# Shortening a decoder's opening from six to four plain tiles, and exchanging two of seven half products in every FFN

## The chip, the cores and the metric

The kernel runs on one core of one Trainium2 chip. The metric is the device time of one execution in microseconds (us), as a median of several runs. A core has five engines that run side by side, each through its own queue in order: PE (TensorE, matmuls and their weight loads), DVE (VectorE), ACT (ScalarE), POOL (GpSimd) and SP (SyncE, which here only issues DMAs). They wait for each other by semaphores.

## What is computed

A decoder trunk of two layers over 512 tokens of width 1024. Each layer has a SwiGLU FFN, a mixer and a second FFN, all with a residual and an RMSNorm ahead of them. Only the FFNs matter here, four in all:

```python
def swiglu(h, w_in, w_out):
    gate, up = jnp.split(h @ w_in, 2, axis=-1)
    return (jax.nn.silu(gate) * up) @ w_out
...
    for l in range(DEPTH):
        x = x + 0.5 * swiglu(rms_norm(x, ffn1_norm[l]), ffn1_w_in[l], ffn1_w_out[l])
        h = rms_norm(x, mix_norm[l]) @ w_mix_in[l]
        ...
        x = x + y @ w_mix_out[l]
        x = x + 0.5 * swiglu(rms_norm(x, ffn2_norm[l]), ffn2_w_in[l], ffn2_w_out[l])
```

The inner width is 2816, that is 22 tiles of 128. Everything is float32. A product is made from three matmuls of rounded parts (high by high, high by low, low by high; mm3, lines 392, 398, 399), so each operand is first split: ACT casts the high part (L378 or L841 for weights, L774/L779 for the moving side), then DVE subtracts it from the source for the low part (L379, L843, L775/L779).

## The kernel before

**An FFN has two stretches.** The first inner tiles are computed plainly while the norm is still being made: the *covered* tiles. Two tiles go together (four PSUM banks: gate and up of each), in four granules of 24 matmuls of 512 columns. Their results stay in the banks until DVE multiplies them by the inverse norm (clear, L643 and L644), ACT takes the silu and DVE the products (values). The opening FFN of layer 0 has six covered tiles, the three others four.

All further tiles go through `halved` (L781), a scheme of seven half products, P1 to P7, in place of eight. A unit is two inner tiles. Each product has 24 matmuls of 256 columns, and the products of a unit share three banks by their letter (L909 to L915):

```python
            new = ("P1", "P2", "P5")
            k = {"P2": "c", "P5": "b", "P3": "b"}.get(p, "a")
            if p in new:
                work[u, k] = bank(kind)
```

So P1, P6, P7 and P4 add into one bank, a; P5 and P3 into b; P2 has c. Between two products of one bank, ACT copies what stands there so far: after P1 (L933), after P6 (g2, L940), after P5 (L943). A product that adds to the bank has to wait for that copy, since it would change what is being read.

**What sets the order.** `plan` (L80) lists all products of an FFN in one order: the seven of each unit in ORDER_IN, and, from the second chunk of units on, products of the output weights (ORDER_OUT) between them by a written pattern. It also gives every DMA and every sum a step. `halved` runs through that list. For each product it emits, in this order: the matmuls; `prepare` of the product three places later (LEAD = 3), whose ACT cast comes first; the copy of the bank; the DVE subtraction of the prepared product; then what the plan and ENTRY have for this step. `follow` pins that order on each engine. The split weights of `prepare` lie in three buffers (tag hl, L839), so the cast for product n + 3 writes to the buffer that product n reads.

ENTRY (L45) is the table of what is emitted at which step around the change from covered tiles to half products: the norm, the normalised input (x), its sums (+), the operands P1 to P7, clears, silus and values. Steps 4 to 7 are the second covered pair's granules, and with four covered tiles, steps 8 to 10 belong to the preparation of the first three products, and step 11 + n follows product n.

Banks come from eight: mm (3), po (1), sc (2), pt (2). Pairs of tiles and units take the sets (mm, mm, mm, po) and (sc, sc, pt, pt) by turns; the units of an FFN take four banks in turn from one set.

**The opening.** At the start PE multiplies zeros (`idle`, L1743) while x and the first weights are on their way: two before x is transposed, one after. Each takes a new tile of the single po bank. The zeros come from a DVE memset (L215), the third of the DVE queue.

Of the kernel before, what the change touches and what calls it, by code (L numbers as in the profile page):

```python
# [8 lines left out]
F32 = mybir.dt.float32  # L9
F32R = mybir.dt.float32r  # L10
# [15 lines left out]
P = 128  # L26
T = 512
D = 1024
# [5 lines left out]
CHUNKS = ((0, 8), (8, 8), (16, 6))  # L34


ORDER_IN = ("P1", "P2", "P6", "P5", "P7", "P3", "P4")
ORDER_OUT = ("P2", "P1", "P5", "P6", "P7", "P3", "P4")
LEAD = 3

# [10 lines left out]
    },  # L51
# [5 lines left out]
    },  # L57
}

# [124 lines left out]
class Trunk:  # L184
# [8 lines left out]
    def __init__(self, ctx, tc):  # L193
        self.tc = tc
        self.nc = tc.nc
        nc = self.nc
        self.const = ctx.enter_context(tc.tile_pool(name="const", bufs=1))
        self.res = ctx.enter_context(tc.tile_pool(name="res", bufs=1))
        self.wp = ctx.enter_context(tc.tile_pool(name="wp", bufs=1))
        self.ps = ctx.enter_context(  # L200
            tc.tile_pool(name="ps", bufs=1, space=bass.MemoryType.PSUM)
        )
        self.dram = ctx.enter_context(
            tc.tile_pool(name="dram", bufs=1, space=bass.MemoryType.DRAM)
        )
        self.ident = self.const.tile([P, P], F32, tag="ident", name="ident")
        make_identity(nc, self.ident)
        self.ones_mean = self.const.tile([P, P], F32, tag="ones_mean", name="ones_mean")
        nc.vector.memset(self.ones_mean, 1.0 / D)
        self.epsc = self.const.tile([P, 1], F32, tag="epsc", name="epsc")  # L210
        nc.vector.memset(self.epsc, EPS)
        self.xT = self.res.tile([P, KD, T], F32, tag="xT", name="xT")

        self.none = self.res.tile([P, T], F32R, tag="inv", name="none")
        nc.vector.memset(self.none.bitcast(F32), 0.0)  # L215

        self.xh, self.xl = [None] * KD, [None] * KD
        self.uid = 0
        self.ntog = 0
        self.tab, self.tab_users = None, []  # L220
        self.chain = {}

    def build_consts(self, scratch):

# [402 lines left out]
    def cover(self, fp, w_in, w_out, covered, mean, begin):  # L627

        nc = self.nc
        if begin is not None:
            x, gain = begin
        A, V = (lambda i, e=e: self.follow(e, i) for e in "av")
        norm, tiles, values = [], [], {}
        halved = self.halved(fp, w_in, w_out, covered, lambda n: deal(n))

        def clear(t):

            gi = fp.tile([P, T], F32, tag="g2", name=self.n("gi"), bufs=2)  # L640
            ui = fp.tile([P, T], F32, tag="u2", name=self.n("ui"), bufs=2)
            pg, pu = tiles[t]
            V(nc.vector.tensor_mul(gi, pg, self.inv))  # L643
            V(nc.vector.tensor_mul(ui, pu, self.inv))  # L644
            values[t] = gi, ui

        def value(t):
            a, k = divmod(t, 4)
            gi, ui = values.pop(t)
            for b in range(2):  # L650
                V(self.hidden(
                    self.quarter(fp, 0, a, b)[:, k, :],
                    *(v[:, 256 * b : 256 * b + 256] for v in (gi, ui)), a != b,
                ))

        def squares():

            norm.append(self.bank("pt" if self.ntog % 2 == 0 else "po"))
            i = self.sum_norm(norm[0])
            if begin is None:  # L660
                self.follow("p", i)

        def deal(n):
            if n == mean and begin is None:
                squares()
            for what in filter(None, ENTRY[covered].get(n, "").split(", ")):
                name, *at = what.split()
                at = [int(v) if v.isdigit() else v for v in at]
                if name == "norm":
                    for e, i in self.take_norm(norm[0], fp):  # L670
                        self.follow(e, i)
                    self.table(SILU)
                    self.signs()
                elif name == "x":
                    self.normalise(fp, *at)
                elif name == "+":
                    x, y = (self.xn[tuple(v)] for v in (at[:2], at[2:]))
                    V(nc.vector.tensor_add(x, x, y))
                elif name == "clear":
                    clear(*at)  # L680
                elif name == "silu":
                    gi = values[at[0]][0]
                    A(self.act(gi, gi, AF.Silu))
                elif name == "values":
                    value(*at)
                elif name == "load":
                    next(halved)
                elif name == "sum":
                    self.first_sum()
                else:  # L690
                    self.operand(fp, name)

        for f in range(0, covered, 2):
            banks = self.next4()

            def parts(k, kk, f=f):
                r = slice(k * P, (k + kk) * P)
                return [w_in[r, f * P : (f + 2) * P], w_in[r, FF + f * P : FF + (f + 2) * P]]

            opening = f == 0 and begin is not None  # L700

            self.stream(
                [(bk, slice(c, c + P), None) for bk, c in zip(banks, (0, 256, 128, 384))],
                parts, self.xact, KD, None,
                (lambda *a: self.open_x(x, gain, fp, *a)) if opening else None,
                None if opening else (lambda k, f=f: deal(2 * f + k // 2)), begin is None or f > 2,

                lead=f == 2 and begin is not None,
            )
            tiles += [banks[:2], banks[2:]]  # L710
            if opening:
                nt = iter(["xh4", "xl4", "xh5", "xl5", "xh6", "xl6", "r2", "r3", "r4", "r5"])
                self.build_consts(lambda dt: fp.tile([P, T], dt, tag=next(nt), name=self.n("c")))

                squares()
        for _ in halved:
            pass
# [997 lines left out]
    def open_x(self, x, gain, fp, k, loaded=False):  # L1715

        if loaded is None:
            if k == 0:
                self.xb[1] = self.turn(self.xb[1], 1)
            self.norm_part(k + 1, fp, self.xb[k + 1], 0)  # L1720
            return
        if not loaded:
            if k == 0:
                self.idle(2)
                self.begin_norm(gain, fp)
                self.table(LNEXP)
                self.follow("a", self.tab_ins)
                self.xb = {0: self.load_x(x, 0, fp)}
                self.load_open(0)
                self.idle(1)  # L1730
                self.xb[1] = self.load_x(x, 1, fp, True)
                self.load_open(1)
            self.norm_part(k, fp, self.xb[k], 0)

            self.between = lambda *a: self.open_x(x, gain, fp, k, None)
            return
        for j in (k + 2, k + 3):
            if j < KD:
                self.xb[j] = self.load_x(x, j, fp)
        for j in (k, k + 1):  # L1740
            self.open_rest(j, fp)

    def idle(self, n):  # L1743

        for _ in range(n):
            b = self.bank("po")
            self.follow("p", self.nc.tensor.matmul(b, self.none[:, :P], self.none, start=True, stop=True))

    def open_rest(self, j, fp):
# [25 lines left out]
def trunk_kernel(  # L1775
# [4 lines left out]
    k = Trunk(ctx, tc)  # L1780
    for l in range(DEPTH):
        k.ffn(
            ffn1_w_in[l], ffn1_w_out[l], mix_norm[l], 4 if l else 6, 2,
            begin=(x, ffn1_norm[0]) if l == 0 else None,
        )
        k.mix(
            l, w_mix_in[l], w_mix_out[l], conv_w[l], hgrn_out_gain[l], fox_q_gain[l],
            fox_k_gain[l], fox_f_bias[l], ffn2_norm[l], hgrn_lb_logits,
        )
        k.ffn(  # L1790
            ffn2_w_in[l], ffn2_w_out[l], ffn1_norm[l + 1] if l + 1 < DEPTH else None, 4, 3,
            out=out if l + 1 == DEPTH else None,
        )
# [29 lines left out]
```

## Time and profile before

| | us |
|---|---|
| median of 3 runs | 1830.18 (1828.83 to 1830.91) |
| the profiled execution | 1832.37 |
| its span, first to last instruction | 1830.6 |
| PE busy | 1821.0 |
| DVE busy | 1445.3 |
| ACT busy | 1001.7 |
| POOL busy | 185.1 |

All times in the profile are of the one profiled execution, counted from the start of its span. A row of a timeline has the start, the time taken (from the first row's start to the last row's end where rows are merged), the engine, the line of the kernel, what is written and read, and in brackets the idle time before it with what ended it. Matmuls overlap: their starts, not their times taken, tell the pace. A row of the waits has who waited for whom, the total, how often, and the longest. In the rows of chains and waits, a name such as "ACT g L940" is the engine, the tile written and the line.

### The profile page before, as it was taken

The numbers are of one execution on the slowest core, as the hardware profiler recorded it, in microseconds if no ns is written. First come the engines' busy times: TensorE is split into PE (matmuls) and PEld (weight loads), VectorE is DVE, ScalarE is ACT, GpSimd is POOL, SyncE is SP. The second block draws the span as 40 slices with busy tenths as digits, with TensorE's granted clock in tenths as the row PEclk, the third lists the DMA queues.
The fourth block names the chain that finished last, engine by engine and source line by source line (L and its number), as shares of the span: only waits on it lengthen the run. The fifth ranks groups of instructions, "written<-read, shape, count | busy, mean of one in ns | idle before, by whom it ended". The sixth has DMA issues, their size and how long they took to land.

```text
span 1830.6 us, 31999 instructions
## 1 busy us (share of the span) xinstructions
PE 1821.0 (99%) x12934; PEld 1674.7 (91%) x12934; DVE 1445.3 (79%) x1965; ACT 1001.7 (55%) x1414; POOL 185.1 (10%) x190
## 2 busy tenths in 40 slices
PE   9999999999999999999999999999999999999999
PEld 7899999888888899999889999998888888999997
DVE  8889786679677888879678887976777778888883
ACT  5455554465666465555445555555656655555552
POOL 0011120100000101112001111201000001020210
PEclk9999999999999999999999999999999999999999
DMA  7668783242543767868276787823425438677762
GB/s 214 177 134 189 177 180 94 68 124 68 127 110 96 216 136 168 193 165 174 81 202 140 174 183 190 163 69 84 114 74 127 119 98 217 161 152 196 154 135 92
DMA packets 249908, 262.38 MB, mean 143 GB/s; under 512 B 19816, under 2 KB 228464, under 8 KB 249760
## 3 DMA queue, kind: packets, MB, share of 16 engines
q1 hardware_dynamic: 193904, 192.15, 35.7%
q0 software_dynamic: 55840, 68.19, 23.4%
q8 instruction: 101, 1.65, 0.4%
q14 instruction: 47, 0.39, 0.1%
q10 hardware_dynamic: 16, 0.00, 0.0%
HBM read 226.15 MB, written 2.17 MB: 125 GB/s over the span
## 4 chain that ended last, share of the span: by engine, by line
PE 96%; ACT 1%; DVE 1%; DMA 1%; issue 0%; SPq 0%; DVEq 0%; ACTq 0%
PE mm L392 14%; PE mm L399 14%; PE mm L398 14%; PE sc L392 6%; PE sc L399 6%; PE sc L398 6%; PE pt L392 6%; PE pt L399 6%; PE pt L398 6%; PE po L392 4%; PE po L399 4%; PE po L398 4%; PE sc L1600 1%; PE po L1655 1%; PE sc L1414 1%; PE pt L1637 1%
## 5 line engine op out<-in xcount | busy, mean ns | idle before, releaser
L841 ACT CAST hl<-w 128x1024 fp32r<-128x1024 f32 x322 | 337.7, 1050 | 347.6 <-PE mm L399 81.9
L843 DVE TENSOR_TENSOR hl<-w,hl 128x1024 fp32r<-128x1024 f32 x322 | 392.5, 1220 | 87.2 <-ACT hl L841 87.0
L379 DVE TENSOR_TENSOR hl<-st,hl 128x1024 fp32r<-128x1024 f32 (+3 forms) x152 | 160.0, 1053 | 120.4 <-ACT hl L378 119.7
L378 ACT CAST hl<-st 128x1024 fp32r<-128x1024 f32 (+3 forms) x152 | 138.6, 912 | 176.3 <-PE po L399 81.5
L392 PE MATMUL mm<-xc,hl 128*128 128x256 f32 (+1 forms) x730 | 201.4, 276 | 0.3 <-ACT g L940 0.3
L399 PE MATMUL mm<-xc,hl 128*128 128x256 f32 x728 | 201.4, 277 | 0.0
L398 PE MATMUL mm<-xc,hl 128*128 128x256 f32 x728 | 201.2, 276 | 0.0
L392 PE MATMUL sc<-xc,hl 128*128 128x256 f32 (+1 forms) x530 | 146.4, 277 | 0.6 <-ACT g L940 0.6
L399 PE MATMUL sc<-xc,hl 128*128 128x256 f32 x528 | 146.1, 277 | 0.0
L398 PE MATMUL sc<-xc,hl 128*128 128x256 f32 x528 | 146.0, 277 | 0.0
L392 PEld LDWEIGHTS mm<-xc,hl 128*128 128x128 f32 x730 | 137.0, 188 | 0.8 <-ACT g L940 0.5
L398 PEld LDWEIGHTS mm<-xc,hl 128*128 128x128 f32 x728 | 136.8, 188 | 0.0
L399 PEld LDWEIGHTS mm<-xc,hl 128*128 128x128 f32 x728 | 136.6, 188 | 0.1
L392 PE MATMUL pt<-xc,hl 128*128 128x256 f32 (+1 forms) x482 | 132.7, 276 | 0.0
L398 PE MATMUL pt<-xc,hl 128*128 128x256 f32 x480 | 132.7, 276 | 0.0
L399 PE MATMUL pt<-xc,hl 128*128 128x256 f32 x480 | 132.6, 276 | 0.0
L392 PE MATMUL mm<-x,hl 128*128 128x512 f32 x272 | 108.8, 400 | 0.0
L399 PE MATMUL mm<-x,hl 128*128 128x512 f32 x272 | 106.1, 390 | 0.0
L398 PE MATMUL mm<-x,hl 128*128 128x512 f32 x272 | 105.9, 389 | 0.0
L392 PEld LDWEIGHTS sc<-xc,hl 128*128 128x128 f32 x530 | 99.5, 188 | 1.5 <-ACT g L940 1.0
L399 PEld LDWEIGHTS sc<-xc,hl 128*128 128x128 f32 x528 | 99.2, 188 | 0.1
L398 PEld LDWEIGHTS sc<-xc,hl 128*128 128x128 f32 x528 | 99.1, 188 | 0.0
(487 smaller groups left out, 5470.6 us busy)
## 6 DMA issues: line engine op xcount, KB each, us to landing
w<-in_ffn_w_in_dram SPq DMA_DIRECT2D x140, 512.0 KB
w<-in_ffn_w_out_dram SPq DMA_DIRECT2D x64, 512.0 KB
w<-in_ffn_w_out_dram POOLq DMA_DIRECT2D x56, 512.0 KB, 9.0
st<-in_w_mix_in_dram SPq DMA_DIRECT2D x80, 256.0 KB
w<-in_ffn_w_in_dram POOLq DMA_DIRECT2D x39, 512.0 KB, 8.1
st<-in_ffn_w_in_dram SPq DMA_DIRECT2D x70, 256.0 KB
w<-S POOLq DMA_DIRECT2D x35, 512.0 KB, 4.7
st<-in_ffn_w_out_dram SPq DMA_DIRECT2D x24, 512.0 KB
```

The source lines that it names most:

```text
L378: a = nc.scalar.copy(hi, src[:, c : c + w])
L379: b = nc.vector.tensor_sub(lo, src[:, c : c + w], hi)
L392: i = nc.tensor.matmul(acc[:, c], ah, bh[:, c], start=first and c.start == 0, stop=False, skip_group_check=True,)
L398: nc.tensor.matmul(acc, ah, bl, start=False, stop=False, skip_group_check=True)
L399: i = nc.tensor.matmul(acc, al, bh, start=False, stop=last, skip_group_check=True)
L841: A(nc.scalar.copy(hi, src))
L843: return lambda: V(nc.vector.tensor_sub(lo, src, hi))
L1414: nc.tensor.matmul(s2[:, :, t], e[:, i * P : (i + 1) * P], e2[:, :, t], start=True, stop=True)
L1600: mm = lambda *a, **k: E(nc.tensor.matmul(*a, skip_group_check=True, **k))
L1637: E(nc.tensor.transpose(tb[:, k * P : (k + 1) * P], to[u][:, j * P : (j + 1) * P], self.ident))
L1655: E(nc.tensor.matmul(self.ob[:, o], half[2][:, j, h].rearrange("p a d -> p (a d)"), part[:, at[0] : at[-1] + 1, :].rearrange("p b t -> p ( ...
```

## The change

It has three parts.

1. *Opening:* layer 0's first FFN has four covered tiles, as the others have; two more tiles go through the half products. It gets a table of its own, "opening", later in its steps than that of the other FFNs: the norm at step 6 (in place of 5), P5's operand at 10, P6's at 11 with the sum that it is made of, P7's at 12, clear 0 at 9 and clear 1 at 11.
2. *Zeros:* four before x is transposed and three after, all of a call into one po bank, and the memset of the zeros comes first on DVE.
3. *Order:* ORDER_IN has P5 ahead of P6, in all four FFNs. ORDER_OUT stays.

```diff
-ORDER_IN = ("P1", "P2", "P6", "P5", "P7", "P3", "P4")
+ORDER_IN = ("P1", "P2", "P5", "P6", "P7", "P3", "P4")
...
-    6: {
-        7: "norm, x 0 0", 8: "x 1 0, clear 0, clear 1", 9: "silu 0, silu 1, x 0 1, P1, + 0 0 0 1",
-        10: "load, P2, values 0, values 1, x 1 1", 11: "P5, clear 2, + 0 0 1 1",
-        12: "silu 2, P6, clear 3, sum", 13: "values 2, silu 3, + 0 1 1 1, P3", 14: "P7, values 3, + 0 0 1 0",
-        15: "P4", 16: "clear 4", 17: "silu 4", 18: "values 4, clear 5", 19: "silu 5", 20: "values 5",
+    "opening": {
+        6: "norm", 7: "load, x 0 0, x 1 0, P1", 8: "x 0 1, + 0 0 0 1, P2", 9: "clear 0, sum",
+        10: "P5, x 1 1", 11: "+ 0 0 1 1, P6, clear 1", 12: "silu 0, + 0 1 1 1, P7", 13: "values 0, P3",
+        14: "silu 1, + 0 0 1 0, P4", 15: "values 1", 17: "clear 2", 18: "silu 2",
+        19: "values 2", 20: "clear 3", 21: "silu 3", 22: "values 3",
     },
...
+        self.none = self.res.tile([P, T], F32R, tag="inv", name="none")
+        self.follow("v", nc.vector.memset(self.none.bitcast(F32), 0.0))
...
-                self.idle(2)
+                self.idle(4)
...
-                self.idle(1)
+                self.idle(3)
...
     def idle(self, n):
 
+        b = self.bank("po")
         for _ in range(n):
-            b = self.bank("po")
             self.follow("p", self.nc.tensor.matmul(b, self.none[:, :P], self.none, start=True, stop=True))
...
-            ffn1_w_in[l], ffn1_w_out[l], mix_norm[l], 4 if l else 6, 2,
+            ffn1_w_in[l], ffn1_w_out[l], mix_norm[l], 4, 2,
```

The change also has `deal` read the new table where the FFN is the opening one.

More of the change, by code (lines that the diff above doesn't have):

```diff
@@ L196, in __init__ @@
         nc = self.nc
+        self.uid = 0
+        self.ntog = 0
+        self.tab, self.tab_users = None, []
+        self.chain = {}
         self.const = ctx.enter_context(tc.tile_pool(name="const", bufs=1))
@@ L208, in __init__ @@
         self.ones_mean = self.const.tile([P, P], F32, tag="ones_mean", name="ones_mean")
-        nc.vector.memset(self.ones_mean, 1.0 / D)
+        self.follow("v", nc.vector.memset(self.ones_mean, 1.0 / D))
         self.epsc = self.const.tile([P, 1], F32, tag="epsc", name="epsc")
@@ L212, in __init__ @@
         self.xT = self.res.tile([P, KD, T], F32, tag="xT", name="xT")
-        self.none = self.res.tile([P, T], F32R, tag="inv", name="none")
-        nc.vector.memset(self.none.bitcast(F32), 0.0)
         self.xh, self.xl = [None] * KD, [None] * KD
[L218 to L221, printed above, removed]
     def build_consts(self, scratch):
@@ L665, in deal @@
                 squares()
-            for what in filter(None, ENTRY[covered].get(n, "").split(", ")):
+            for what in filter(None, ENTRY[covered if begin is None else "opening"].get(n, "").split(", ")):
                 name, *at = what.split()
```

## The prediction

> **What bounds the kernel now.** I read the page's busy shares first.
>
> ```profile
> PE 1821.0 (99%) x12934; PEld 1674.7 (91%) x12934; DVE 1445.3 (79%) x1965; ACT 1001.7 (55%) x1414; POOL 185.1 (10%) x190
> ```
>
> PE has work for 1821.0 of 1830.6 us. Whatever stops PE is added to the time almost whole, and only less work on PE, or fewer stops, takes time away. So I looked next at the view of the waits, for who stops PE now (total us, times, longest):
>
> ```profile
> PE sc L392 <- ACT g L940: 0.6, 2, 0.3
> ...
> PE mm L392 <- ACT g L940: 0.3, 1, 0.3
> ```
>
> These two of its nine rows decide this case: three times already a half product waits for L940, the copy of bank a that ACT makes after P6. One of the three lies in layer 0's second FFN. The timeline of PE there, with one product's start from its first FFN ahead:
>
> ```profile
> 109.08 0.28 PE L392 MATMUL sc<-m,hl 128*128 128x256 f32 x1
> ...
> 643.33 0.28 PE L392 MATMUL sc<-xc,hl 128*128 128x256 f32 x1
> ...
> 646.05 0.28 PE L392 MATMUL pt<-xc,hl 128*128 128x256 f32 x1
> ...
> 649.24 0.38 PE L392 MATMUL sc<-xc,hl 128*128 128x256 f32 x1 [0.31 <-ACT g L940]
> ...
> 652.08 0.28 PE L392 MATMUL pt<-xc,hl 128*128 128x256 f32 x1
> ```
>
> That of ACT at the same two places, and of DVE at the second:
>
> ```profile
> 109.32 1.05 ACT L841 CAST hl<-w 128x1024 fp32r<-128x1024 f32 x1
> 110.28 0.59 ACT L943 ACTIVATE u<-mm 128x512 f32<-128x512 f32 x1
> ...
> 646.72 1.03 ACT L779 CAST xc<-xn 128x1024 fp32r<-128x1024 f32 x1
> 647.66 1.04 ACT L841 CAST hl<-w 128x1024 fp32r<-128x1024 f32 x1
> 648.60 0.58 ACT L940 ACTIVATE g<-sc 128x512 f32<-128x512 f32 x1
> ```
>
> ```profile
> 643.75 0.68 DVE L643 TENSOR_TENSOR gi<-pt,inv 128x512 f32<-128x512 f32 x1
> 644.35 0.68 DVE L644 TENSOR_TENSOR ui<-pt,inv 128x512 f32<-128x512 f32 x1
> 644.95 0.68 DVE L936 TENSOR_TENSOR g<-g,sc 128x512 f32<-128x512 f32 x1
> 645.54 1.22 DVE L843 TENSOR_TENSOR hl<-w,hl 128x1024 fp32r<-128x1024 f32 x1
> 647.78 1.23 DVE L779 TENSOR_TENSOR xc<-xn,xc 128x1024 fp32r<-128x1024 f32 x1 [1.02 <-ACT xc L779]
> 648.93 1.22 DVE L843 TENSOR_TENSOR hl<-w,hl 128x1024 fp32r<-128x1024 f32 x1
> 650.06 1.22 DVE L678 TENSOR_TENSOR xn<-xn,xn 128x1024 f32<-128x1024 f32 x1
> ```
>
> P6 starts at 643.33, P5 at 646.05, 2.72 later, and P7, due at 648.77, only at 649.24. It writes to bank a, which L940 still reads until 649.18. ACT was late here because the weight cast L841 stands ahead of L940. P5 lies between P6 and P7 and covers the copy almost entirely.
>
> **The change, part by part.**
>
> *The exchange makes P6 and P7 neighbours.* With P5 ahead of P6, the order of a unit is P1 P2 P5 P6 P7 P3 P4. In the first two units of each FFN nothing stands between P6 and P7. From the plan's patterns, written out, an output product falls between them in four of the seven later units and none in three (the fourth, sixth and ninth unit). That makes 5 of 9 units, in 4 FFNs: 20 neighbouring pairs. Before, there was always at least one product between. Both use bank a, and in the order of the changed program's instructions the first matmul of every P7 waits for L940, and L940 stands directly behind an L841 in all 36 units. That L841 casts for the product three places after P6 into the buffer that P6 reads, so it can't begin before P6 has ended.
>
> What PE then waits through, by the rows above. A product takes 646.05 - 643.33 = 2.72. The buffer's release reaches ACT 109.32 - 109.08 = 0.24 after the next product starts. The cast holds ACT for 0.95 (109.32 to 110.28, 647.66 to 648.60). From L940's start to PE's start are 0.64 (648.60 to 649.24). And the product that starts after such a stop is slower by 0.12 (649.24 to 652.08 is 2.84). Sum: 0.24 + 0.95 + 0.64 + 0.12 = **1.95 per pair**. Nothing covers it: PE is in order, P3 and P4 stand behind P7, and DVE and ACT have nothing to do for PE that it lacked. Where an output product stands between, 0.24 + 0.95 + 0.64 = 1.83 fits into its 2.72 and costs nothing. 19 of the pairs at 1.95 are +37.1; the twentieth is in the opening, below.
>
> *P5 is a product earlier and meets its bank too early.* The third bank of the units' set is still held by the second covered tile until clear 1 reads it (L643, gi<-pt). Before, P5 was the fourth product, at 646.05. Now it is the third, due at 643.33, and L643 ends at 643.75 + 0.68 = 644.43; with 0.06 to PE (649.18 to 649.24) it starts at 644.49: 1.16 late, with 0.12 for the restart 1.28. The order of DVE around it has the same steps in the changed program. In three FFNs: +3.8. In turn the three old waits for L940 go, since ACT is free again by the end of P6: 3 x (0.47 + 0.12) = -1.8.
>
> *The opening waits longer at both places.* Its table puts clear 1 behind P6's operand on DVE. From the end of P1 on, in order: 0.24 to the cast of P6's weights; 1.06 from a cast's start to the DVE step that it feeds (646.72 to 647.78); 1.15 for that L843 (647.78 to 648.93 for an equal step); 1.25 for the sum L678 until ACT can begin; 1.06 for the cast of P6's operand; 1.15 for its low part; 0.68 for L643; 0.06. This is 6.65 after the end of P1, and P5 is due 2.72 after it: 3.93 late, 4.05 with the restart. (L678's 1.22 is in the last row of DVE's.)
>
> P7's operand comes behind that on the same two engines. From P5's start, 0.74 after L643 began: DVE has L643, L644 and L936 (0.60 each, 643.75 to 645.54 for three), L843 (1.14, 648.93 to 650.06), L678 done at 3.42; ACT then casts that operand, P3's weights, copies P5's bank (L943, 0.49 until the next), casts P3's operand and P4's weights, 4 x 0.95 + 0.49, and starts L940 at 7.74, so P7 at 8.38. It was due at 2.84 + 2.72 = 5.56: 2.82 late, 2.94 with the restart. Opening: **+7.0**, the twentieth pair in it.
>
> *Less work on PE.* The third covered pair had 96 matmuls of 512 columns; its unit has 7 x 24 = 168 of 256 columns. Pace of the wide ones: the 80 steps between these rows, (78.22 - 60.08) / 80 = 0.2268.
>
> ```profile
> 60.08 0.39 PE L398 MATMUL sc<-x,hl 128*128 128x512 f32 x1
> ...
> 78.22 0.39 PE L392 MATMUL pt<-x,hl 128*128 128x512 f32 x1
> ```
>
> 96 x 0.2268 = 21.77 against 7 x 2.72 = 19.04: **-2.7**. The unit also adds seven casts and seven subtractions to ACT and DVE and takes away four each; both have room in the FFN, 55% and 79% busy. With two pairs in place of three, every later stage also takes the other set of banks; the old waits for L940 are 0.3 on sc and 0.3 on mm, so I cost that at nothing (bounds -0.5 and +0.5). Of DMAs, a unit's four raw weights and its sums on POOL come in place of the pair's eight halves.
>
> ```profile
> w<-S POOLq DMA_DIRECT2D x35, 512.0 KB, 4.7
> ```
>
> The exchange moves POOL's sums by a step: the second sum (w<-S) lands 4.7 after issue, and the plan leaves it three products (8.2) or more until P3's cast, so I cost it at nothing; if it came late it would hold ACT ahead of L940, the long rival below.
>
> *The zeros.* PE starts slow:
>
> ```profile
> 1.62 1.65 PE L1747 MATMUL po<-none 128*128 128x512 f32 x2 [1.62 <-DVE none L215]
> ...
> 3.80 1.11 PE L1768 MATMUL mm<-ident,xs 128*128 128x128 f32 x4 [0.33 <-DMA xs<-in_x_dram]
> 4.56 0.77 PE L1747 MATMUL po<-none 128*128 128x512 f32 x1
> 6.35 1.22 PE L445 MATMUL sc<-x,hl 128*128 128x512 f32 x2 [1.01 <-ACT hl L378]
> 7.37 1.05 PE L445 MATMUL pt<-x,hl 128*128 128x512 f32 x2
> 8.22 1.05 PE L1768 MATMUL mm<-ident,xs 128*128 128x128 f32 x4
> ...
> 11.63 0.91 PE L445 MATMUL pt<-x,hl 128*128 128x512 f32 x2
> ```
>
> Until about 12 each pair of L445 takes 0.85 (7.37 to 8.22), 0.43 a matmul against 0.23 later. Over the twelve L445 and one round of transposes the slow pace costs 12 x 0.2 + 0.4 = 2.8. The full pace comes some 5.9 after the dense work begins at 6.35. The zeros were two in 1.65, with pauses; now four in 4 x 0.43 = 1.7, from about 1.4 on, and three in 1.3 after the transposes, to about 5.9. They start nothing late: x comes at 3.8, and L445 waits for ACT until 6.35. So dense work begins two to five us earlier, and the full pace may come as much earlier. Bounds 0 and -2.8; nothing in the trace says which, so I take the middle, **-1.4**.
>
> The Trainium skill (TensorE: Matmul & The Clock Gate, Part 1) says that the clock is raised after a busy window of about 3.4 us that runs free of the kernel's start; the 5.9 here lies between one and two such windows, which agrees, and by the rule the gain would differ from run to run. The same part warns of the reverse, a half clock after a window of idleness; it speaks against this change, as the fourth rival.
>
> **Sum**, against the profiled execution's 1832.4: 37.1 + 7.0 + 3.8 - 1.8 - 2.7 - 1.4 = **+42.0**, so 1874.4. The median of the runs shown, 1830.2, is 2.2 below that execution, and what is predicted is such a median: **1872.2**.
>
> **The rivals.**
>
> *Short pairs.* If L940 came without the cast ahead of it, a pair would cost 1.95 - 0.95 = 1.00, and 19 of them 18 less: 1854. For it: ACT is only 55% busy. Against it: 647.66 and 648.60 show the cast ahead, and the order is pinned. 6%.
>
> *Long pairs.* In the fourth, sixth and ninth unit the cast ahead of L940 is that of P3's weights, which waits for the second sum's DMA. If it came half a product late there, 12 x 1.36 = 16 more: 1888.5. For it: that DMA is issued behind others on POOL. Against it: 8.2 or more of lead for 4.7. 7%.
>
> *No waits, faster.* L940 and P7 could be free of each other, if P6's copy were out of the way by the time P7 is due. It decides at one point: whether the path from P6's end to L940's end is under 0.3, the time by which matmuls overlap. Then the pairs and the three old waits cost nothing, clear 1 is in time by the same slack, and less work is left: 1830.2 - 1.8 - 2.7 - 1.4 = 1824.3. Against it stand the 0.94 of L841 and the 0.64 behind it. 3%.
>
> *The clock falls in the opening.* PE stands still for 3.9 ahead of P5 and 2.8 ahead of P7. If its pace were halved for the 5.9 that the raise took at the start, PE would lose half of that, 2.9: 1875.1. Against it: the first pause here is a one-off of 3.9, and the trace shows no fall of the pace anywhere, nor a pause as long. 14%.
>
> *The zeros do nothing*: 1873.6, within the forecast.
>
> **How the numbers follow.** Forecast 70%, short 6, long 7, faster 3, clock 14. The range takes in the zeros' bounds (-1.4, +1.4), the opening and P5's bank from half to one and a half of 10.8 (-5, +5), and the fall of the clock: 1863 to 1883. It leaves out the short, the long and the faster case. The last is all that falls below 1830; about 0.2% (3.7 us) is what a measurement of this kernel can tell from no change: faster 0.03, same 0.01, slower 0.96.
>
> **What would show it.** In the waits of PE after: L392 <- ACT g L940 some 20 times, about 1.8 each and near 37 in all; L392 <- DVE gi L643 four times, one near 3.9. In the timeline, P6, then L841 0.24 after its end, L940, P7. The page: PE about 97% busy. Wrong would be: L940's waits in all 36 units, or few; or a slow pace of PE after the opening's stop.

## The result, and the profile after

The changed kernel takes **1891.82 us** (median of four runs, 1886.24 to 1894.97); the kernel before, on the same chip, 1829.93 (1828.83 to 1830.91). The ratio is **1.0335**, with a 95% interval of 1.031 to 1.036. The forecast was 1872.2 with a range of 1863 to 1883: the direction was right, and the size was 19.6 us short.

The profiled execution of the changed kernel took 1891.33 with a span of 1889.6. That is 59.0 more than the span before, where the terms of the forecast gave 42.0. So 17.0 us are to be found in the trace. The other 2.6 of the miss are no work: the forecast took 2.2 off for the median, and this profiled execution lies 0.5 below its median.

The engines' row of the page after:

```profile
PE 1832.0 (97%) x13010; PEld 1686.8 (89%) x13010; DVE 1455.2 (77%) x1967; ACT 1005.5 (53%) x1420; POOL 187.4 (10%) x192
```

PE is busy 97% of the span, as foretold, but of a longer span. By the forecast it has 2.7 us less to do than before (fewer wide matmuls, more narrow ones), and yet it is busy for 11.0 us more: its work got slower, which no wait shows. First the waits of PE (who waited for whom, total us, times, longest):

```profile
PE sc L392 <- ACT g L940: 15.9, 9, 3.4
PE pt L392 <- ACT g L940: 15.7, 6, 3.6
PE pt L392 <- DVE gi L643: 6.1, 3, 3.9
PE mm L392 <- ACT g L940: 5.0, 3, 1.7
PE po L392 <- ACT g L940: 4.4, 2, 2.7
...
PE mm L392 <- DVE gi L643: 1.1, 1, 1.1
```

L940 is waited for 9 + 6 + 3 + 2 = 20 times, the number of the forecast, and L643 four times, once for 3.9. The new thing stands in the last column: 3.4, 3.6 and 2.7 are no stops of the ordinary kind. An ordinary one, in the timelines of ACT and PE:

```profile
146.97 1.04 ACT L841 CAST hl<-w 128x1024 fp32r<-128x1024 f32 x1
147.92 0.59 ACT L940 ACTIVATE g<-sc 128x512 f32<-128x512 f32 x1
```

```profile
148.56 0.38 PE L392 MATMUL sc<-xc,hl 128*128 128x256 f32 x1 [1.68 <-ACT g L940]
```

This is the chain that was forecast, cast, copy, product: 0.95 from cast to copy, 0.64 from copy to PE. The bracket counts from the modelled end of the last matmul, 0.28 after its start, where the next would have been due 0.11 after it; with 0.17 for that and 0.12 for the restart a stop of 1.68 costs 1.97, where the forecast had 1.95. A long one, 61 us later in the sixth unit of the same FFN (POOL, ACT, PE):

```profile
199.56 0.89 POOL L859 DMA_DIRECT2D w<-S  x1 [22.73 <-DVE S L829]
```

```profile
207.97 1.04 ACT L841 CAST hl<-w 128x1024 fp32r<-128x1024 f32 x1 [1.88 <-DMA w<-S]
208.92 0.59 ACT L940 ACTIVATE g<-pt 128x512 f32<-128x512 f32 x1
```

```profile
209.57 0.39 PE L392 MATMUL pt<-xc,hl 128*128 128x256 f32 x1 [3.61 <-ACT g L940]
```

The cast ahead of L940 is that of P3's weights, and they come by the second sum's DMA. It was issued at 199.56, after a DVE sum, and let the cast go at 207.97, 8.4 later; the cast had waited 1.88 for it. The order of the instructions is as ordinary, but the cast itself is late, and the copy behind it with it.

What happens after such a stop is seen in the view by windows: pairs of neighbouring stretches of 3.41 us, each pair with a stop in its first one. The columns are the stretch, its length, busy time and instructions of PE, PEld, DVE, ACT and POOL, then PE's granted clock, and the share and rate of the DMAs.

```profile
60.72:64.13 3.41, 0.00 (x0) 0.00 (x0) 2.30 (x4) 1.99 (x2) 0.00 (x0) 1.00 1.18 238
64.13:67.55 3.42, 3.21 (x15) 3.25 (x16) 3.42 (x5) 1.15 (x2) 0.00 (x0) 0.50 0.44 141
146.05:149.47 3.42, 1.74 (x16) 1.55 (x15) 3.42 (x4) 2.39 (x3) 0.00 (x0) 1.00 1.08 236
149.47:152.88 3.41, 3.41 (x33) 3.41 (x32) 2.33 (x4) 1.05 (x1) 1.28 (x1) 1.00 0.60 182
207.50:210.91 3.41, 1.34 (x11) 1.34 (x12) 1.88 (x2) 1.54 (x2) 0.00 (x0) 1.00 1.17 248
210.91:214.32 3.41, 3.41 (x18) 3.41 (x18) 0.22 (x1) 0.29 (x1) 0.00 (x0) 0.50 0.99 334
798.00:801.41 3.41, 0.79 (x7) 0.80 (x8) 2.44 (x3) 1.54 (x2) 0.00 (x0) 1.00 1.17 220
801.41:804.83 3.42, 3.42 (x19) 3.42 (x18) 0.00 (x0) 0.00 (x0) 0.00 (x0) 0.50 1.09 367
```

After the stop of 1.68 the clock stays at 1.00, and 33 matmuls fit into the next stretch. After the others it is 0.50, and 15 to 19 fit. There are six such stretches in the execution, from 64.13, 74.37, 210.91, 801.41, 1142.75 and 1736.67: behind both stops of the opening and behind the sixth unit's stop in each of the four FFNs. They start on one grid of 3.413 us, whatever the program does, and the mean clock says the same: half of 6 x 3.413 us is 10.2 us' worth of clock, and without it a span of 1889.6 has a mean of 0.995.

So my theory is this. The order costs what was forecast at its 14 ordinary stops. To that come a second sum that is too late in the sixth unit, and half a clock for 3.4 us wherever PE has stood still for the larger part of a stretch of the grid. The rivals: the 17 us come from the opening; every stop costs more than it seems; or the slow stretches come from the DMAs, which are dense in most of those places (shares up to 1.18 in the rows).

### The profile page after: what moved, and what is told of

Its sections match the earlier page's. It is cut to its first block, busy times and chain, and to the rows that moved or that the text cites. A ratio compares the mean times of both kernels' runs of the same rounds, so it can differ in the third digit from the quotient of the medians.

```text
span 1889.6 us, 32191 instructions
## 1 busy us (share of the span) xinstructions
PE 1832.0 (97%) x13010; PEld 1686.8 (89%) x13010; DVE 1455.2 (77%) x1967; ACT 1005.5 (53%) x1420; POOL 187.4 (10%) x192
## 5 line engine op out<-in xcount | busy, mean ns | idle before, releaser
L843 DVE TENSOR_TENSOR hl<-w,hl 128x1024 fp32r<-128x1024 f32 x328 | 400.9, 1223 | 95.8 <-ACT hl L841 94.9
L392 PE MATMUL sc<-xc,hl 128*128 128x256 f32 (+1 forms) x795 | 220.9, 279 | 15.9 <-ACT g L940 15.9
L392 PE MATMUL pt<-xc,hl 128*128 128x256 f32 x723 | 202.9, 281 | 21.7 <-ACT g L940 15.7
L398 PE MATMUL sc<-xc,hl 128*128 128x256 f32 x792 | 219.8, 278 | 0.0
L399 PE MATMUL sc<-xc,hl 128*128 128x256 f32 x792 | 219.7, 277 | 0.0
L398 PE MATMUL pt<-xc,hl 128*128 128x256 f32 x720 | 202.0, 281 | 0.0
L399 PE MATMUL pt<-xc,hl 128*128 128x256 f32 x720 | 201.8, 280 | 0.0
L392 PEld LDWEIGHTS sc<-xc,hl 128*128 128x128 f32 x795 | 149.9, 189 | 18.0 <-ACT g L940 17.8
L392 PEld LDWEIGHTS pt<-xc,hl 128*128 128x128 f32 x723 | 137.9, 191 | 23.4 <-ACT g L940 16.8
L398 PEld LDWEIGHTS sc<-xc,hl 128*128 128x128 f32 x792 | 149.7, 189 | 0.0
L399 PEld LDWEIGHTS sc<-xc,hl 128*128 128x128 f32 x792 | 149.2, 188 | 0.0
L392 PE MATMUL mm<-m,hl 128*128 128x256 f32 x504 | 139.9, 278 | 0.0
L398 PE MATMUL mm<-m,hl 128*128 128x256 f32 x504 | 139.8, 277 | 0.0
L399 PE MATMUL mm<-m,hl 128*128 128x256 f32 x504 | 139.7, 277 | 0.0
L398 PEld LDWEIGHTS pt<-xc,hl 128*128 128x128 f32 x720 | 138.2, 192 | 0.0
L399 PEld LDWEIGHTS pt<-xc,hl 128*128 128x128 f32 x720 | 137.8, 191 | 0.0
L392 PE MATMUL mm<-xc,hl 128*128 128x256 f32 (+1 forms) x393 | 108.7, 277 | 6.1 <-ACT g L940 5.0
L392 PE MATMUL mm<-x,hl 128*128 128x512 f32 x272 | 108.8, 400 | 0.0
L398 PE MATMUL mm<-xc,hl 128*128 128x256 f32 x392 | 108.3, 276 | 0.0
```

Source lines behind the costliest of these rows:

```text
L392: i = nc.tensor.matmul(acc[:, c], ah, bh[:, c], start=first and c.start == 0, stop=False, skip_group_check=True,)
L398: nc.tensor.matmul(acc, ah, bl, start=False, stop=False, skip_group_check=True)
L399: i = nc.tensor.matmul(acc, al, bh, start=False, stop=last, skip_group_check=True)
L843: return lambda: V(nc.vector.tensor_sub(lo, src, hi))
```

## The experiments

### The order alone

The edit to the kernel before:

```diff
-ORDER_IN = ("P1", "P2", "P6", "P5", "P7", "P3", "P4")
+ORDER_IN = ("P1", "P2", "P5", "P6", "P7", "P3", "P4")
```

> The kernel before with the new ORDER_IN alone. Theory (the order carries nearly all of the loss, the opening little): the three later FFNs are those of the changed kernel, which were longer by 17.1, 12.7 and 11.3 us from squares to squares; the first FFN, which has eight units here, gets the stop of the pairs as well, about 4 of 1.95 and one of 3.6 to 3.9 with a window of half clock of 1.6 behind it: 13 to 14. In all +54, 1884 us (1878 to 1889). PE shows a granted clock of a half for 3.4 us behind the sixth unit's stop in each FFN and nowhere else. Rival (the opening and its new table cost the 17 us that the forecast lacked): only 19 x 1.95 + 3.8 - 1.8 = +39 is left, 1869.

Measured: 1887.15 (1884.94 to 1888.1), the kernel before beside it 1831.36; ratio 1.031 (1.0292 to 1.0327). The theory holds and the opening as the main cause is out: the exchange alone brings 55.8 of the 62 us. It has six stretches of half clock in four places, all behind the stop of the unit of inner tiles 14 and 15 (3.6, 4.9, 3.8 and 3.5), which is the sixth, or the fifth in the first FFN with its six covered tiles; after the two middle ones the clock stays down for two stretches. One of them:

```profile
796.01 0.58 PE L392 MATMUL pt<-xc,hl 128*128 128x256 f32 x1 [4.92 <-ACT g L940]
```

### The opening without the order

The edit to the changed kernel:

```diff
-ORDER_IN = ("P1", "P2", "P5", "P6", "P7", "P3", "P4")
+ORDER_IN = ("P1", "P2", "P6", "P5", "P7", "P3", "P4")
```

> The changed kernel with the old ORDER_IN. Theory: no pair of neighbours is left, so none of the 14 stops of 1.68 and none of the four of 2.7 to 3.6. Of the opening stay the 2.2 us gained up to the first squares and the 2.7 of covered work, and one stop: P6 comes third and its operand is ready about 0.7 ahead of the clear that P5 waited for, so about 3.2 in place of 3.9, with a window of half clock (1.6) behind it; P5 and P7 are then late by under 1. In all +4 + 1.6 - 2.7 - 2.2 = about +1, 1831 us (1827 to 1834). Rival (the opening carries the 17 us that the forecast lacked): 1830 + 17 + 5 = about 1850.

Measured: 1839.08 (1838.24 to 1839.35), ratio 1.0044 (1.0029 to 1.0059). It is far from the rival's 1850, but 8 above my number. PE's stops in the opening:

```profile
62.48 0.38 PE L392 MATMUL sc<-xc,hl 128*128 128x256 f32 x1 [1.94 <-ACT xc L779]
63.73 0.58 PE L398 MATMUL sc<-xc,hl 128*128 128x256 f32 x1 [0.88 <-DVE xc L779]
72.71 0.38 PE L392 MATMUL sc<-xc,hl 128*128 128x256 f32 x1 [1.85 <-ACT g L940]
```

P6 is late by 1.94 + 0.88, about the 3.2 expected. P7's 1.85 was expected under 1, and there are two stretches of half clock, not one; the second follows a stretch in which PE was busy for 1.55 of 3.41:

```profile
70.40:73.81 3.41, 1.55 (x13) 1.36 (x13) 1.75 (x4) 1.75 (x3) 0.00 (x0) 1.00 0.00 0
73.81:77.23 3.42, 3.42 (x18) 3.42 (x18) 3.31 (x3) 1.82 (x4) 0.00 (x0) 0.50 0.02 5
```

This pair counts against the DMAs as a cause: their share is 0.00 there, and the clock falls all the same. From the opening's squares (L551) to the mixer's the first FFN takes 320.3 here and 315.2 before: 5.0 more, although its covered work is 2.7 less. The start is 2.1 shorter, and 2.5 more lie in layer 1's mixer; more on that below.

### The copy ahead of the cast

The edit to the changed kernel:

```diff
             product(u, p, acc, p in new, p in ("P2", "P3", "P4"), n in (0, 7))
+            if kind == "I" and p == "P6":
+                work[u, "g2"] = g2 = tmp("g2")
+                A(nc.scalar.activation(g2, acc, AF.Copy, scale=-1.0))
             rest = prepare(*seq[n + LEAD]) if n + LEAD < len(seq) else None
...
             elif p == "P6":
-                work[u, "g2"] = g2 = tmp("g2")
-                A(nc.scalar.activation(g2, acc, AF.Copy, scale=-1.0))
+                pass
```

> The changed kernel with the copy L940 emitted ahead of the weight cast L841 behind P6. Theory: the stop of a pair loses the cast's 0.95, so 14 x 0.95 = 13.3 less; in the sixth units the copy no longer stands behind a cast that waits for the second sum's DMA, so their four stops of 13.35 in all become 4 x 0.73, 10.4 less; these are then too short to halve the clock, and four windows of about 1.55 go, 6.2 less; the opening's P7 waits 0.95 less. In all -31: 1861 us (1856 to 1867). Rival 1 (the four slow stretches behind the sixth units are not the stop's doing): they stay, 1867. Rival 2 (the copy waits for PE or for its operand buffers, not for the cast): 1892, stops of 1.68 as before.

Measured: 1857.6 (1856.6 to 1864.17), ratio 1.0154 (1.0135 to 1.0173). The same place in its timelines (L920 is the copy here):

```profile
144.65 0.60 ACT L920 ACTIVATE g<-sc 128x512 f32<-128x512 f32 x1
145.15 1.04 ACT L841 CAST hl<-w 128x1024 fp32r<-128x1024 f32 x1
```

```profile
145.30 0.39 PE L392 MATMUL sc<-xc,hl 128*128 128x256 f32 x1 [0.69 <-ACT g L920]
```

Copy and cast have changed places, and the stop is 0.99 shorter. The four sixth units now stop for 0.69 each, and one stretch of half clock is left, behind the opening's P5. Both rivals are out: 1892 by 34, and 1867, without the clock, by 9.

### The second sum a product earlier

The edit to the changed kernel's plan:

```diff
-            m = split["P6"] - 1
+            m = split["P6"] - 2
```

> The changed kernel with the plan's second sum one product earlier, where it stood in the kernel before. Theory: the DMA of the second sum in the sixth units lands before P3's weights are cast, the four stops there fall from 13.35 in all to 4 x 1.68 (6.6 less), and with stops of 1.68 the clock is not halved there (four windows of about 1.55, 6.2 less): 1879 us (1875 to 1884), with two windows of half clock left, both in the opening. Rival 1 (the slow stretches have another cause than the long stop): 1885. Rival 2 (the landing is late because POOL's queue is full, whatever the step of the sum): 1892.

Measured: 1875.34 (1874.53 to 1877.06), ratio 1.0245 (1.0229 to 1.026). POOL, ACT and PE in the sixth unit of the first FFN:

```profile
197.40 0.89 POOL L859 DMA_DIRECT2D w<-S  x1 [19.90 <-ACT hl L841]
```

```profile
206.99 1.04 ACT L841 CAST hl<-w 128x1024 fp32r<-128x1024 f32 x1 [1.62 <-PE pt L399]
```

```profile
208.59 0.38 PE L392 MATMUL pt<-xc,hl 128*128 128x256 f32 x1 [1.63 <-ACT g L940]
```

The DMA is issued 2.2 earlier, the cast no longer waits for it but for PE, as in every other unit, and the stop is 1.63. No clock falls in the sixth units any more; the three stretches of half clock that are left are in the opening. The time fell by 0.9% of before, 16.5 us, even more than the 12.8 of stops and clock; by the rival without the clock it would have been 6.6. The rest, 3.7, is less than the interval of the changed kernel's ratio leaves open. It is also about what the changed kernel's profiled execution lost in a stretch of the second FFN (804 to 900) in which matmuls came every 0.118 us in place of 0.113 at a full granted clock. There is no such stretch here or in the changed kernel when it was run again, but two shorter ones in the kernel before (284 to 308 and 1764 to 1792, about 1 us each); I have no cause for them.

### Zeros in the stops

The edit to the changed kernel; zz is a small tile of zeros, read by broadcast:

```diff
+        def fill(b, n):
+            for _ in range(n):
+                self.follow("p", nc.tensor.matmul(
+                    b[:, :256], self.zz[:, 0:1].to_broadcast([P, P]), self.zz[:, 0:1].to_broadcast([P, 256]), start=False, stop=False, skip_group_check=True
+                ))
...
+            if kind == "I" and p == "P7" and seq[n - 1][2] == "P6" and seq[n - 1][0] == "I":
+                fill(work[u, "b"], 28 if w == 14 else 24 if begin and w == 4 else 12)
+            if kind == "I" and p == "P5" and w == 4 and begin:
+                fill(work[u, "a"], 28)
             product(u, p, acc, p in new, p in ("P2", "P3", "P4"), n in (0, 7))
```

> The changed kernel with zeros multiplied and added to a bank of the unit in the stops: 12 matmuls of 256 columns (12 x 0.113 = 1.36 us) ahead of P7 where P6 stands just ahead of it, 28 in the sixth units, 24 and 28 in the opening. The products and the result are the same. Theory (the granted clock falls where PE stands still for more than about half of a 3.4 us window): the stops stay as long as they were, PE is busy in them, no window of half clock is left after the start, and about 9.2 us go: 1882 us (1878 to 1886). Rival 1 (the slow stretches behind the long stops come from the DMAs or from what follows, not from PE standing still): 1892, with the slow stretches still there. Rival 2 (the stop is shortened by PE being warm, or lengthened by the zeros' own queue): under 1875 or over 1895.

Measured: 1885.04 (1882.46 to 1889.3), before 1830.7; ratio 1.0299 (1.0285 to 1.0314). This was only half a success. Two stretches of half clock were left in its profiled execution. One is in the opening, since the zeros ahead of P7 went to a bank that ACT was still to read:

```profile
73.24 1.15 PE L882 MATMUL pt<-zz 128*128 128x256 f32 x5 [2.58 <-ACT u L955]
```

The other follows a sixth unit in which the DMA came later than the zeros lasted:

```profile
1141.96:1145.37 3.41, 1.62 (x14) 1.42 (x13) 1.23 (x1) 1.54 (x2) 0.00 (x0) 1.00 1.11 314
1145.37:1148.78 3.41, 3.41 (x18) 3.41 (x17) 0.29 (x1) 0.36 (x1) 0.00 (x0) 0.50 0.64 193
```

In the three other sixth units the same DMAs ran and the clock stayed, since PE was busy. The time lies between theory and rival, nearer to the theory, and the run by itself would not decide. Its profiled execution also has a stretch of slow matmuls at full clock like the one above (212 to 308), which cost it 3.6.

### Longer stops

The edit to the changed kernel:

```diff
             elif p == "P6":
                 work[u, "g2"] = g2 = tmp("g2")
-                A(nc.scalar.activation(g2, acc, AF.Copy, scale=-1.0))
+                for _ in range(3):
+                    A(nc.scalar.activation(g2, acc, AF.Copy, scale=-1.0))
```

> The changed kernel with the copy L940 made three times over, so that each pair's stop is longer by two copies, 2 x 0.49 = 0.98. Theory (a 3.4 us window of which PE stands still for more than about 54% is followed by one of half clock): the 14 ordinary stops grow from 1.68 to about 2.65; such a stop fills more than 54% of a window for about 7 in 10 of the positions that the window can have against it, so 9 to 10 new windows of half clock at 1.55 come with it: 19 x 0.98 = 18.6 and 15, 1925 us (1916 to 1934). Rival (the falls come from something special to the opening and the sixth units, not from the length of a stop): 18.6 alone, 1910, and the windows of half clock stay six.

Measured: 1958.45 (1955.34 to 1963.02), ratio 1.07 (1.0685 to 1.0714). The rival is out by 48; the theory was too low by 33. The two extra copies cost 1.25, not 0.98, so the 14 ordinary stops are 2.93 long, and the clock fell behind all 14 of them, not 10; behind three of the four sixth units, the opening's P7 and one ordinary pair it fell for two stretches. The longer stops (19 x 0.27) and the 19 new stretches in place of 9 to 10 make about 20 of those 33; I have not placed the rest. One ordinary place:

```profile
98.00:101.41 3.41, 0.83 (x7) 0.83 (x8) 1.85 (x3) 2.99 (x5) 0.00 (x0) 1.00 0.85 269
101.41:104.82 3.41, 3.41 (x19) 3.41 (x18) 0.00 (x0) 0.00 (x0) 0.00 (x0) 0.50 0.48 161
```

The mean clock of this execution is 0.978, which is 25 stretches (25 x 3.413 / 2 / 1953.5 = 0.022). A stop of 1.68 has no such price and one of 2.93 has it every time, in the same places of the program.

### Both causes away, and the changed kernel again

The changed kernel with the earlier sum and the zeros as above, and this edit to the zeros' place:

```diff
-                fill(work[u, "b"], 28 if w == 14 else 24 if begin and w == 4 else 12)
+                fill(work[u, "c"], 24 if begin and w == 4 else 12)
```

> The changed kernel with both corrections that the runs so far point to: the second sum one product earlier, so that the sixth units' stops are 1.68 like the others (this alone gave 1875.3), and zeros multiplied in all stops, those ahead of the opening's P7 now in P2's bank, which nothing reads at that time. The products and the result are the same. Theory: no window of half clock is left after the start; of the 1875.3 go the opening's windows (3.9 in the profiled run with the earlier sum): 1871.4 us (1868 to 1875), what the forecast's own terms give (1872.2). Rival (the forecast's terms were wrong by more than the late sums and the clock, and only chance brought the runs near): the stops' total in the profile differs from 19 x 1.95 + 7.0 + 3.8 by more than 3, or the time stays at 1875 or above.

> The changed kernel unchanged, in the same call as the one without windows of half clock. Theory: 1886 to 1896 as before, with five to eight windows of half clock, whose number depends on where the 3.4 us windows lie against the six long stops; a run with a lower mean granted clock is a longer one. Rival (the spread of the changed kernel comes from its DMAs): the time does not go with the granted clock.

Measured: 1874.22 (1873.67 to 1876.3), ratio 1.0243 (1.0229 to 1.0257), for the first; 1894.69 (1892.53 to 1896.96), ratio 1.0355 (1.0341 to 1.0369), for the second. The cores' view of the first, and of the second:

```profile
core 0: 1872.5 us, clock 1.000
```

```profile
core 0: 1890.8 us, clock 0.993
```

With the second sum in time and the clock never down, the kernel takes 2.0 more than the forecast and 20.5 less than the changed kernel beside it. By the starts of matmuls its stops and restarts add up to 50.2, where the forecast's terms for them (19 x 1.95 + 7.0 + 3.8) make 47.9. That is within the 3 that the rival needed, and the time lies 0.8 below the rival's 1875, so the rival is out, if narrowly: the terms for the order were sound, and the two causes make most of the rest. Two things fell short. Against the kernel with the earlier sum alone almost nothing was gained (1.0243 and 1.0245), although its stretches of half clock in the opening are gone. From squares to squares the first FFN is 2.1 shorter than there, not 3.9; one reason is under point 4 below. The start (0.8), layer 0's mixer (1.4) and what follows the last squares (0.9) are longer and layer 1's mixer is 2.3 shorter, without a cause that I know. And the spread of the changed kernel's runs doesn't follow the granted clock, as the theory had it: that was 0.991 to 0.995 in the five, and the run with 0.995 (1893.46) took longer than one with 0.993 (1892.53). What makes the spread stays open.

### The zeros, alone and with the copy first

The first is the kernel before with the change's zeros and nothing else. The second also has the copy ahead of the cast, by the edit shown above.

> The kernel before with the zeros' part alone: memset first, four and three zeros into one bank each. Theory: the clock is granted in full from about 6 us on in place of 12.24, and the first squares come 2.2 us sooner, as in the changed kernel (31.99 in place of 34.17); nothing else moves: 2.2 less than before in the same call, a ratio of 0.9988. Rival (the earlier start in the changed kernel came from its new opening, not from the zeros): ratio 1.000.

> The kernel before with the zeros' part and with the copy L940 ahead of the weight cast L841; the order of the half products and the opening stay as before. Theory: 2.2 less by the zeros, and the three waits for L940 of 0.3 each with their restart of 0.12, 1.3, go: 3.5 less than before, a ratio of 0.9981, 1827 us. Rival (the cast that now comes 0.5 later makes the operand of the product after the next late): at or above before.

Measured: zeros alone 1829.13 against 1830.7, ratio 0.9992 (0.9983 to 1.0000); with the copy 1829.57, ratio 0.9993 (0.9984 to 1.0002). The zeros gain about 1.6, at the edge of what can be told. PE's pace in the opening shows that the mechanism is the one expected:

```profile
6.38 0.73 PE L444 MATMUL sc<-x,hl 128*128 128x512 f32 x2 [0.48 <-ACT hl L377]
...
7.76 0.71 PE L444 MATMUL sc<-x,hl 128*128 128x512 f32 x2
8.31 0.63 PE L444 MATMUL pt<-x,hl 128*128 128x512 f32 x2
8.78 0.62 PE L444 MATMUL sc<-x,hl 128*128 128x512 f32 x2
```

A pair of wide matmuls takes 0.47 here (8.31 to 8.78), where it took 0.85 before at the same time. The copy first gained nothing in the old order. The three waits for L940 went, and these came instead:

```profile
PE sc L391 <- DVE u L947: 1.8, 2, 0.9
...
PE mm L391 <- DVE u L947: 0.9, 1, 0.9
```

The rival was right in kind: the cast that comes later pushes DVE's steps back, and P4 waits 0.9 for DVE to read P7's bank, where P7 had waited 0.3 for ACT.

### Four covered tiles with the other FFNs' table

The edit to the changed kernel, which also has the old ORDER_IN:

```diff
-            for what in filter(None, ENTRY[covered if begin is None else "opening"].get(n, "").split(", ")):
+            for what in filter(None, ENTRY[covered].get(n, "").split(", ")):
```

> The changed kernel with the old ORDER_IN and with the opening on the table of the three other FFNs, whose norm stands at step 5 in place of 6, a granule of 5.4 us earlier: four covered tiles and the zeros' part are what is left of the change. Theory (the opening's two stops of 2.8 and 1.9 and their windows of half clock, 3.2, in the kernel with the old order come from the table's lateness, not from having four covered tiles): both stops and both windows go, the covered work's 2.7 and the zeros' 1.6 stay, and the mixer of layer 1 keeps the 2 that it lost in every kernel with four covered tiles and this start: 1839.1 - 4.7 - 3.2 = 1831 us or a little less, within 0.2% of before. Rival (the norm can't be had a granule earlier: DVE and ACT are still busy with the opening): PE stops at the first half products or in the second covered pair as long as before, 1836 to 1840 or above.

Measured: 1833.03 (1831.93 to 1834.91), ratio 1.0012 (1.0003 to 1.0021). The norm can be had a granule earlier, and the clock stays up, but two stops remain:

```profile
62.52 0.38 PE L386 MATMUL sc<-xc,hl 128*128 128x256 f32 x1 [1.56 <-ACT g L927]
69.70 0.39 PE L386 MATMUL sc<-xc,hl 128*128 128x256 f32 x1 [1.45 <-ACT g L934]
```

With their restarts they cost 3.6, more than the 2.7 of covered work that is saved. Of all versions only the two with the zeros and the old opening and order reach below the kernel before, and by hardly more than can be measured.

## Why the forecast was right in sign and wrong in size

By the spans (+59.0 measured, +42.0 forecast), step by step:

| step of the forecast | forecast | measured |
|---|---|---|
| 14 ordinary pairs x 1.95 | 27.3 | 27.3 |
| four pairs in sixth units | 7.8 | 14.0 |
| the last pair | 1.95 | 1.1 |
| opening, P5 and P7 | 7.0 | 9.2 |
| P5's bank in three FFNs | 3.8 | 4.1 |
| half clock (five stretches not counted above) | 0 | 7.6 |
| start, up to the first squares | -1.4 | -2.2 |
| covered work | -2.7 | -2.8 |
| old waits for L940 | -1.8 | -1.8 |
| mixers | 0 | +2.1 |
| matmuls' pace at full clock | 0 | +2.0 |

The measured column is from starts of matmuls: a stop by how late the next matmul starts against the pace, half clock by what the 24 matmuls behind a stop then lose (the sixth stretch, behind the opening's P5, lies within P7's lateness). It adds up to 60.6, so 1.6 too much; some small stops of before that are gone are not in it.

1. **The exchange** was right: the number of stops, the chain in them, and 1.95 for each of the 14 that are 1.68 by the bracket. The kernel with the copy first shows that the cast is 0.99 of it.

2. **"The second sum (w<-S) lands 4.7 after issue, and the plan leaves it three products (8.2) or more until P3's cast, so I cost it at nothing"** failed in both numbers. The lead was 6.5, not 8.2: the DMA was issued at 199.56, and the cast could have begun at about 206.1 (207.97 less the wait of 1.88). The plan had moved the sum one product closer to its user. And the landing took 8.3, with the DMAs' share at 0.92 in that time; the 4.7 was a median over 35 in the kernel before. In the sixth unit of layer 0's second FFN this DMA landed in 4.7 there (issued at 792.05; share 0.68 until it landed) and in 8.3 after (790.62; 0.89). So the place wasn't slow before: with the new order the DMA runs there beside denser ones. The forecast named this as the rival "long pairs", with three kinds of unit and 1.36 each; it was one kind, and by the brackets 1.66 each: (3.61 + 3.60 + 2.73 + 3.41) - 4 x 1.68 = 6.6. The earlier sum took it away.

3. **"The clock falls in the opening"** was a rival with 14%, for one place and at 2.9. It was no rival but a term of the sum: six places, about 1.5 each in the five that cost something by themselves. What failed is the reason against it, that the trace before shows no fall: that trace has no stop after the start over 0.5, so it could not show one. Longer and shorter stops turned the fall on and off.

4. **The opening's P7, "so P7 at 8.38"** after P5's start (its terms add up to 8.35), came at 74.94 - 64.34 = 10.60. Nearly all of these 2.2 stand in one row of ACT. L943, the copy of P5's bank, was counted as 0.49 and not as something that waits:

```profile
71.91 0.60 ACT L943 ACTIVATE u<-pt 128x512 f32<-128x512 f32 x1 [1.96 <-DVE hq L731]
```

L943 writes to a tile with two buffers, and the clears had taken both; it waits until "values 0" on DVE has read one. Since ACT sets P7's start here, one slow stretch behind P5 costs nothing by itself. In the kernel without any half clock P7 (75.92) comes 10.68 after P5 (65.24) too:

```profile
65.24 0.39 PE L394 MATMUL pt<-xc,hl 128*128 128x256 f32 x1 [0.66 <-DVE gi L645]
...
75.92 0.39 PE L394 MATMUL sc<-xc,hl 128*128 128x256 f32 x1 [2.28 <-ACT g L952]
```

With two such stretches, in the kernel with the earlier sum, P7 comes 11.40 after P5. Put into that kernel, the zeros therefore gained 0.7 up to P7 and, with the clock up behind it, about 1.5.

5. **P5's bank** was right: the bracket's 1.10 is a matmul that starts 1.26 late, where 1.16 had been forecast. So were the covered work and the old waits. The zeros' -1.4 was within its bounds: -2.2 in the changed kernel, about -1.6 alone.

6. **Not settled** are 2 us in layer 1's mixer. It took 258.3 before. Of the kernels with four covered tiles it took 260.1 to 260.9 in six (the changed kernel's two runs among them) and 259.2 in one, but 257.9 and 258.0 in the two with zeros in the stops. In the first seven PE waits there for a DMA, 0.5 to 1.4 us, and in the last two and the kernel before it does not. Why that DMA comes later is open. The wait in the changed kernel:

```profile
PE sc L1600 <- DMA A<-b: 1.1, 1, 1.1
```

## What to carry to other kernels

A stop of PE has two prices, its length and, from about half of a 3.4 us window on, half the clock in the next one; so when two products change places, look for the longest stop that it makes and not only for the mean one. A wait that an engine has in one place is inherited by all that stands behind it in its queue: before costing a copy at its own length, follow the cast or DMA ahead of it in each kind of unit, with the slowest landing (7.2 in the kernel before, more than the lead of 6.5) and not the median. And an edit that takes a wait away shows its worth only in the order in which it will run: the copy ahead of the cast gave 34 us in the new order and nothing in the old one.

## What the runs showed of the hardware

The clock's fall needs no idle window. PE was busy for 1.55 and 1.62 us of a 3.41 us window that was followed by half clock (rows above), and for 1.61, 1.64 and 1.74 in ones that were not. The two that are not above, from the kernels with the copy first and with the order alone:

```profile
59.15:62.56 3.41, 1.61 (x15) 1.41 (x13) 2.36 (x2) 1.48 (x4) 0.00 (x0) 1.00 1.10 214
62.56:65.97 3.41, 1.33 (x11) 1.36 (x12) 3.31 (x5) 1.28 (x3) 0.00 (x0) 1.00 1.08 269
```

```profile
1664.24:1667.65 3.41, 1.64 (x15) 1.44 (x14) 3.41 (x4) 2.49 (x3) 0.00 (x0) 1.00 1.18 225
1667.65:1671.06 3.41, 3.41 (x30) 3.41 (x31) 2.87 (x4) 0.39 (x1) 0.60 (x1) 1.00 0.43 141
```

The line lies at 1.6 us of busy PE (as the profile models it), 47% of the window. All windows of the 13 profiles agree, from the first one at full clock on: each of the 48 at full clock with less than 1.6 us of busy PE was followed by half clock, and none of the about 7000 with more than 1.65. A window at half clock needs more to end it: with up to 2.58 us of busy PE (ten windows) the clock stayed down, and with 2.85 or more (39 windows) it came back. The Trainium skill (TensorE: Matmul & The Clock Gate, Part 1) puts the half clock behind a whole idle window of about 3.4 us that runs free of the kernel. The grid and the length agree with these runs; that the window must be idle does not: a stop of 1.85 was enough, and one of 1.68, 49% of a window at most, never was.

A second one: DMAs of one kind and size landed 4.7 us after issue in the median before, in the place that mattered 8.3 after, and in the median of the changed kernel 6.5, though it moves only one more of them:

```profile
w<-S POOLq DMA_DIRECT2D x36, 512.0 KB, 6.5
```
